# Copies of the running sum moved from the start of a down run into the duo ahead of it, and a sixth raw weight tile in a decoder trunk's feed-forward stage

## The chip, the core and the metric

The kernel runs on one core of a Trainium2 chip. Its engines are named as in the profile: PE (matrix products), PEld (PE's loading of the stationary operand), DVE (vector), ACT (scalar), POOL, and SP, whose queue issues the loads. The metric is the time of one execution of the whole program in microseconds (us): 2176.53 is the median of three runs of the kernel before (2175.78 to 2177.68).

## The reference, cut to what matters

A decoder trunk of two layers over 256 tokens of width 2048, in float32. Each layer has a mixer (gated linear attention in the first, differential attention over a shared K/V in the second) and a SwiGLU feed-forward stage, the FFN, with 5632 inner columns. The change touches the FFN, which runs twice:

```python
def swiglu(h, w_gate_up, w_down):
    gate, up = jnp.split(h @ w_gate_up, 2, axis=-1)
    return (jax.nn.silu(gate) * up) @ w_down
...
        f = swiglu(rmsnorm(x, pre_ffn_g[i]), ffn_w_gate_up[i], ffn_w_down[i])
        x = x + rmsnorm(f, post_ffn_g[i])
```

## The kernel before

**Numbers.** A float32 weight tile of 128x1024 is loaded by SP (`load`, L271) into one of NRAW = 5 buffers named `raw`. It is split into two parts: `hi`, a cast by ACT (L306), and `lo`, the rest, by DVE (L309). A product of a 128x128 piece of activations with a 128x512 piece of weights is three matmuls: hi by hi, hi by lo, lo by hi (L419 to L421 in `mm_act`, L559 to L561 in `triple`). Each `hi`/`lo` pair lies in a ring of NRING = 9, and `pump` keeps the splitting at most that far ahead of what PE has given free.

**Up steps.** The 5632 columns are 11 chunks of 512, numbered 0 to 10. Chunk 0 is done by `gated_first`. Each of the other ten is a *duo* (`gated_duo`, which calls `duo_seeded`): the gate chunk and the up chunk are worked together, in a scheme in which six of the eight slices of the depth (four in chunk 1) need seven products in place of eight. Such a fast slice is four weight parts, a to d, made by DVE additions (L341) of two raw tiles; part d is 128x512 and lies in narrower buffers, `hi5` and `lo5`, which take turns with two rooms in a spare tile (`self.narrow = (fp, 2, 2)`: four places in all). The sums of the duo stand in PSUM banks, which the code numbers 0 to 7. Behind the last fast slice, `early` takes the sums apart: ACT copies bank 0 into `sg` (L1270), and DVE does four additions (L1259), one of which writes into bank 7. The slices that are left (1 and 7) follow as plain products, and `late` finishes each bank as it is done.

**Down steps.** `ffn_steps` sets the order: up chunks in groups of two, with a down run of two output chunks behind most of them. A down run (`down_act`) multiplies the gated columns of one group with `w_down` and adds to what earlier groups gave. That running sum stands in SBUF, in `f`. So each output chunk begins with two copies by ACT, one for each half of the tokens, from `f` into two fresh PSUM buffers (L472), and the matmuls add onto these. At its end, ACT copies the sums back (L1335). The first group has no such copies. Of the down runs that have them, eight in each FFN stand behind a duo.

**What sets the order.** The code is recorded in the order in which it is written; then a scheduler sets the order on each engine, with priorities (`urgent`) and ties (`behind`: not ahead of a given instruction). On the chip each engine takes its own row in order: what stands behind a waiting instruction waits as well. SP's loads too are one row.

**Memory.** `fp` is a pool that is open during one FFN and lies where the mixer's pool lay before. PSUM has six buffers named `acc` and two named `tp`.

Of the kernel before, what the change touches and what calls it, by code (L numbers as in the profile page):

```python
# [11 lines left out]
F32 = mybir.dt.float32  # L12
# [6 lines left out]
P = 128  # L19
# [29 lines left out]
NRAW, NRING = 5, 9  # L49
# [147 lines left out]
class Trunk:  # L197
    def __init__(self, ctx, tc, t):
        self.ctx, self.tc, self.nc, self.t = ctx, tc, tc.nc, t

        def pool(name, **kw):
            return ctx.enter_context(tc.tile_pool(name=name, bufs=1, **kw))

        self.const = pool("const")
        self.big = pool("big")
        self.ring = pool("ring")
        self.hs = pool("hs")
        self.psum = pool("psum", space=bass.MemoryType.PSUM)
        self.dram = pool("dram", space=bass.MemoryType.DRAM)
        self.n = 0  # L210
        self.later = []
        self.stream = weight_stream()
        self.loads = load_list(self.stream)
        self.n_used = self.n_done = 0
        self.subs = {}
        self.split_off = None
        self.parts = {}
        self.raws = {}
        self.n_dma = self.n_conv = self.n_take = self.n_free = 0
        self.pool_lo = set()  # L220
        self.n_narrow = 0
        self.cap = 2
        self.ident = self.const.tile([P, P], F32, tag="ident", name="ident")
# [43 lines left out]

    def load(self):
        name, idx = self.loads[self.n_dma]
        raw = self.ring.tile([P, 1024], F32, tag="raw", name=self.uid("raw"), bufs=NRAW)  # L270
        self.nc.sync.dma_start(raw, self.t[name][idx])  # L271
        self.raws[self.n_dma] = raw
        self.n_dma += 1
# [28 lines left out]
    def split(self, src, gp=False):  # L302
        nc = self.nc
        w = src.shape[-1]
        hi, lo = self.places(w)
        cast = nc.scalar.copy(hi, src)  # L306
        eng = nc.gpsimd if gp else nc.vector
        with self.past(self.split_off):
            rest = eng.tensor_tensor(out=lo, in0=src, in1=hi.bitcast(F32), op=ALU.subtract)  # L309
        if not gp:  # L310
            self.parts[self.n_conv] = cast.ins, rest.ins
        return hi, lo
# [66 lines left out]

    def pump(self):  # L380
        n = len(self.stream)
        while self.n_conv < min(n, self.n_free + NRING, self.n_take + self.cap):
            self.convert()
            while self.n_dma < min(len(self.loads), self.n_done + NRAW):
                self.load()

    def take(self, name, idx, kind="plain"):
# [74 lines left out]
    def down_act(self, aT, w, s0, order, ns, evac, skew=0, base=None):  # L462

        ps, taken = {}, {}

        def run(u, b):
            c, s = order[u]
            if c not in ps:
                ps[c] = [self.acc(), self.acc()]
                if base:  # L470
                    for i in range(2):
                        self.nc.scalar.copy(ps[c][i], base(c, i))  # L472
            if not b:
                taken[u] = self.take(w, (c, s0 + s))
            self.mm_act(ps[c][b], aT, b, s, taken[u], ns, base is not None)
            if s == ns - 1:
                evac(c, b, ps[c][b])
            if b:
                self.free()
            self.tick()  # L480

        n = len(order) - skew
        for u in range(n):
            run(u, 0)
            run(u, 1)
        for b in range(2):
            for u in range(n, len(order)):
                run(u, b)

    def duo_seeded(self, aT, forms, fast, chunks, early, late):  # L490

        ps, held = {}, []
        (w1, n1), (w2, n2) = chunks

        def bank_of(bank):
            if bank not in ps:
                ps[bank] = self.tp().rearrange("p j t -> p (j t)") if bank in (2, 6) else self.acc()
                return True
            return False

        def add(bank, a, wp, j, last, onto=False):
            first = bank_of(bank)
            self.triple(ps[bank], a, wp, j, first and not onto, last, onto)

        def plain(bank, s, b, wp, last, onto=False):
            for j in range(2):
                add(bank, aT.tokens(2 * s + j, b), wp, j, last and j == 1, onto)
            if last:
                with self.behind(LATE_BEHIND):
                    late(bank, ps)  # L510
            self.tick()

        for s in range(7):
            k1, k2 = 2 * s, 2 * s + 1
            if s not in fast:
                wp = self.take(w1, (n1, s))
                for b, bank in enumerate((1, 3)):
                    plain(bank, s, b, wp, False)
                self.free()
                held.append(s)  # L520
                continue
            f, last = forms.pairs.index(s), s == fast[-1]
            plan = {
                "a": ((0, aT.tokens(k1, 0)), (1, aT.tokens(k2, 0))),
                "b": ((6, forms.fast(f, 2)), (2, forms.fast(f, 3))),
                "c": ((5, forms.fast(f, 1)), (3, aT.tokens(k2, 1))),
                "d": ((4, forms.fast(f, 0)),),
            }
            for kind, prods in plan.items():
                wp = self.take("duo", (*chunks, s), kind)  # L530
                for j, (bank, a) in enumerate(prods):
                    add(bank, a, wp, j, last and bank in (0, 4, 5, 6))
                self.free()
                if kind != "d":
                    self.tick()
            if last:
                bank_of(7)
                with self.behind(EARLY_BEHIND):
                    self.urgent(early)(ps)
        kept = [(s, self.take(w2, (n2, s))) for s in held]  # L540
        for s, wp in kept:
            plain(2, s, 0, wp, False)
        wp = self.take(w1, (n1, 7))
        for b, bank in enumerate((1, 3)):
            plain(bank, 7, b, wp, True)
        for s, wp2 in kept:
            plain(7, s, 1, wp2, False, True)
            self.free()
        self.free()
        wp = self.take(w2, (n2, 7))  # L550
        plain(2, 7, 0, wp, True)
        plain(7, 7, 1, wp, True, True)
        self.free()
# [696 lines left out]
        self.defer(5, lambda: next_gain(3))  # L1250
        self.chunk_act(aT, w, 3, 8, self.urgent(evac(3)), tail=SKEW)

    def gated_duo(self, hT, forms, w, c, rs, new_sg):

        nc = self.nc
        made = []
# [28 lines left out]
            else:  # L1285
                gated(1, ps[bank])

        self.duo_seeded(hT, forms, ffn_pairs(c), ((w, c), (w, 11 + c)), early, late)
        return made[0]

    def ffn(self, fp, hT, rs, gi, wgu, wd, post, after, name, reload, side=None):
        nc = self.nc
        self.narrow, self.n_narrow = (fp, 2, 2), 0
        forms = Forms(FAST_FFN, range(8), self.whole(4, [P, 4, 2, 4, P], f"{name}_fast", F32R))
        self.rest_of(forms, 2 * gi + 1, f"{name}_rest")
        temp = self.whole(5, [P, 4, C], f"{name}_temp")
# [45 lines left out]
        def part(c, b):  # L1342
            return f[0][:, b, c * C : (c + 1) * C]

        f = []
        plan = ffn_steps()
        for n, (kind, which, *chunks) in enumerate(plan):
            if kind == "up":
                sg = self.gated_duo(hT, forms, wgu, which, rs, new_sg) if which else gated_first()
                follow = plan[n + 1]  # L1350
                wait = 4 if which else 1
                if follow[0] == "down" and which not in follow[1]:
                    wait = 2 * len(down_order(*follow[1:])) + 1
                self.defer(wait, lambda sg=sg, c=which: gate_T(sg, c))
                continue
            chunks, skew = chunks[0], 0
            if not f:
                f.append(self.whole(5, [P, 2, D], name))
                if side:
                    self.defer(5, side)  # L1360
            if which == last:
                if chunks[0] == 0:
                    reload()
                else:
                    skew = LAST_SKEW
                for c in chunks:
                    gains[c] = self.gain(post, c)

            def done(c, b, ps, grp=which):
                if skew:  # L1370
                    self.urgent(evac)(grp, c, b, ps)
                else:
                    with self.behind(DOWN_BEHIND):
                        evac(grp, c, b, ps)

            base = None if which == first else part
            self.down_act(gTs[which], wd, 2 * which[0], down_order(which, chunks), 2 * len(which), done, skew, base)

    def values(self, vp, aT, rs, i, steps, every):

# [348 lines left out]
```

## Time and profile before

| | |
|---|---|
| runs of the kernel before, median (lowest to highest) | 2176.53 us (2175.78 to 2177.68) |
| the profiled execution | 2176.25 us |
| its span, first to last instruction | 2174.5 us |
| granted PE clock, mean | 0.999 |
| first FFN, second FFN, about | 385 to 1094 us, 1468 to 2174 us |
| raw loads of `w_gu`, of `w_d` | 352 and 176, 512 KB each, median 4.4 and 4.5 us to landing |
| ACT copies L472 | 80, 580 ns each (median) |

In rows of the timeline, the first two numbers are start and duration in us, then come engine, line, operation, output and inputs, and how many were merged; brackets hold the idle time of the engine ahead of it and what ended it. In rows of the waits stand the total, how often, and the longest. A matmul of 512 columns is drawn 0.39 us long, but the next one starts 0.23 us after it, so that rows of PE overlap.

### The profile page before, as it was taken

How to read it: one execution, taken by the hardware profiler on the slowest of the kernel's cores; microseconds unless marked ns; L12 is line 12 of the kernel's file. 1: busy time of each engine (PE TensorE's matmuls, PEld its weight loads, DVE VectorE, ACT ScalarE, POOL GpSimd, SP SyncE). 2: the span in 40 equal slices, each digit the busy share in tenths (PEclk: the TensorE clock that was granted, in tenths of full speed). 3: DMA queues.
4: the chain of work that ended last, by engine and by line, in shares of the span. 5: the costliest groups of instructions: out<-in, count | busy, mean ns of one | idle time of the engine just before them, and what ended most of it. 6: DMA issues, size and time to landing. Idle time of an engine off the chain costs nothing.

```text
span 2174.5 us, 28418 instructions
## 1 busy us (share of the span) xinstructions
PE 2153.9 (99%) x10044; PEld 1785.0 (82%) x10044; DVE 1942.6 (89%) x2666; ACT 1376.5 (63%) x1926; POOL 38.4 (2%) x66
## 2 busy tenths in 40 slices
PE   9999999999999999999999999999999999999998
PEld 7888788888888888888878888888888888888876
DVE  7989988999999999999798567889999999999996
ACT  8756655666666666666776455566656666666664
POOL 1000000000000000000000000000000000000000
PEclk9999999999999999999999999999999999999999
DMA  8545566566555666656767555465655556566664
GB/s 309 166 150 192 176 225 214 208 220 231 174 191 205 213 213 209 207 181 214 249 203 244 188 172 163 149 235 186 228 202 185 188 200 209 202 210 205 210 215 154
DMA packets 125043, 440.08 MB, mean 202 GB/s; under 512 B 14091, under 2 KB 16820, under 8 KB 123620
## 3 DMA queue, kind: packets, MB, share of 16 engines
q1 hardware_dynamic: 123724, 436.44, 59.3%
q10 hardware_dynamic: 1176, 1.84, 0.2%
q8 instruction: 78, 1.28, 0.2%
q14 instruction: 65, 0.53, 0.1%
HBM read 429.82 MB, written 9.97 MB: 202 GB/s over the span
## 4 chain that ended last, share of the span: by engine, by line
PE 88%; DVE 5%; DMA 3%; ACT 2%; issue 1%; SPq 0%; POOL 0%; ACTq 0%; DVEq 0%; POOLq 0%
PE acc L419 11%; PE acc L421 11%; PE acc L420 11%; PE acc L560 10%; PE acc L561 10%; PE acc L559 10%; PE acc L707 8%; PE acc L708 4%; PE tp L561 3%; PE tp L560 3%; PE tp L559 3%; DMA raw<-in_w_d_dram 2%; DVE lo L309 2%; ACT hi L306 2%; DVE raw L341 1%
## 5 line engine op out<-in xcount | busy, mean ns | idle before, releaser
L309 DVE TENSOR_TENSOR lo<-raw,hi 128x1024 fp32r<-128x1024 f32 x921 | 1098.4, 1218 | 131.3 <-ACT hi L306 125.8
L306 ACT CAST hi<-raw 128x1024 fp32r<-128x1024 f32 x923 | 946.9, 1051 | 376.5 <-PE acc L707 89.6
L419 PE MATMUL acc<-hi,f_ffn_gT 128*128 128x512 f32 x704 | 270.5, 392 | 6.1 <-ACT acc L472 6.0
L420 PE MATMUL acc<-lo,f_ffn_gT 128*128 128x512 f32 x704 | 272.6, 389 | 0.0
L421 PE MATMUL acc<-hi,f_ffn_gT 128*128 128x512 f32 x704 | 270.5, 389 | 0.0
L560 PE MATMUL acc<-lo,h_ffn 128*128 128x512 f32 x612 | 239.2, 391 | 0.1
L561 PE MATMUL acc<-hi,h_ffn 128*128 128x512 f32 x612 | 238.4, 390 | 0.0
L559 PE MATMUL acc<-hi,h_ffn 128*128 128x512 f32 x612 | 227.7, 389 | 0.0
L419 PEld LDWEIGHTS acc<-hi,f_ffn_gT 128*128 128x128 f32 x704 | 132.1, 188 | 38.6 <-ACT acc L472 11.1
L341 DVE TENSOR_TENSOR raw<-raw 128x512 f32<-128x512 f32 x232 | 159.2, 686 | 3.3
L421 PEld LDWEIGHTS acc<-hi,f_ffn_gT 128*128 128x128 f32 x704 | 132.2, 188 | 27.5
L420 PEld LDWEIGHTS acc<-lo,f_ffn_gT 128*128 128x128 f32 x704 | 132.2, 188 | 27.2
L560 PEld LDWEIGHTS acc<-lo,h_ffn 128*128 128x128 f32 x612 | 114.9, 188 | 26.2 <-DVE lo L309 1.0
L559 PEld LDWEIGHTS acc<-hi,h_ffn 128*128 128x128 f32 x612 | 114.9, 188 | 24.1
L561 PEld LDWEIGHTS acc<-hi,h_ffn 128*128 128x128 f32 x612 | 114.9, 188 | 23.1
L306 ACT CAST hi<-sum 128x512 fp32r<-128x512 f32 x72 | 44.8, 622 | 96.6 <-DVE sum L341 96.6
L306 ACT CAST f_ffn_rest<-sum 128x512 fp32r<-128x512 f32 x56 | 34.9, 623 | 95.6 <-DVE sum L341 95.6
L707 PE MATMUL acc<-h_q,hi 128*128 128x512 f32 x256 | 92.5, 401 | 0.0
L707 PE MATMUL acc<-h_kv,hi 128*128 128x512 f32 x256 | 90.7, 399 | 0.0
L707 PE MATMUL acc<-h_mix,hi 128*128 128x512 f32 x256 | 90.5, 398 | 0.0
L1335 ACT COPY f_ffn<-acc 128x512 f32<-128x512 f32 x80 | 46.7, 586 | 56.6 <-PE acc L421 56.1
L341 DVE TENSOR_TENSOR sum<-raw,raw 128x512 f32<-128x512 f32 x116 | 79.3, 683 | 0.1
(417 smaller groups left out, 4105.8 us busy)
## 6 DMA issues: line engine op xcount, KB each, us to landing
raw<-in_w_gu_dram SPq DMA_DIRECT2D x352, 512.0 KB, 4.4
raw<-in_w_d_dram SPq DMA_DIRECT2D x176, 512.0 KB, 4.5
raw<-in_gla_w_r_dram SPq DMA_DIRECT2D x32, 512.0 KB, 4.4
raw<-in_gla_w_v_dram SPq DMA_DIRECT2D x32, 512.0 KB, 4.0
raw<-in_gla_w_out_dram SPq DMA_DIRECT2D x32, 512.0 KB, 4.8
raw<-in_w_v_dram SPq DMA_DIRECT2D x32, 512.0 KB, 4.5
raw<-in_w_k_dram SPq DMA_DIRECT2D x32, 512.0 KB, 4.3
raw<-in_diff_w_q_dram SPq DMA_DIRECT2D x32, 512.0 KB, 3.5
```

The lines of the kernel that those rows point to most:

```text
L306: cast = nc.scalar.copy(hi, src)
L309: rest = eng.tensor_tensor(out=lo, in0=src, in1=hi.bitcast(F32), op=ALU.subtract)
L341: return self.nc.vector.tensor_tensor(out=out, in0=in0, in1=in1, op=ALU.add)
L419: nc.tensor.matmul(ps, ah, rh, start=(kt == 0 and not onto), stop=False, skip_group_check=onto)
L420: nc.tensor.matmul(ps, ah, rl, start=False, stop=False, skip_group_check=onto)
L421: nc.tensor.matmul(ps, al, rh, start=False, stop=(kt == 2 * ns - 1), skip_group_check=onto)
L559: nc.tensor.matmul(ps, ah, wh, start=first, stop=False, skip_group_check=onto)
L560: nc.tensor.matmul(ps, ah, wl, start=False, stop=False, skip_group_check=onto)
L561: nc.tensor.matmul(ps, al, wh, start=False, stop=last, skip_group_check=onto)
L707: nc.tensor.matmul(ps, lh, aT.both(kt), start=(kt == 0), stop=False)
L708: nc.tensor.matmul(ps[:, SEQ:], ll, aT.hi(kt), start=False, stop=(kt == KT - 1))
L1335: nc.scalar.copy(fc, ps)
```

## The change

The diff, without the lines that only pass an argument on:

```diff
     def load(self):
         name, idx = self.loads[self.n_dma]
-        raw = self.ring.tile([P, 1024], F32, tag="raw", name=self.uid("raw"), bufs=NRAW)
+        pool, bufs = self.ring, NRAW
+        if self.more_raw and name[:3] in ("w_g", "w_d"):
+            self.n_more += 1
+            if self.n_more % (NRAW + 1) == 0:
+                pool, bufs = self.more_raw, 1
+        raw = pool.tile([P, 1024], F32, tag="raw", name=self.uid("raw"), bufs=bufs)
...
-        cast = nc.scalar.copy(hi, src)
+        with self.past(self.led):
+            cast = nc.scalar.copy(hi, src)
...
     def pump(self):
         n = len(self.stream)
-        while self.n_conv < min(n, self.n_free + NRING, self.n_take + self.cap):
+        while self.n_conv < min(n, self.n_free + NRING, self.n_take + self.cap, self.open_to or n):
             self.convert()
-            while self.n_dma < min(len(self.loads), self.n_done + NRAW):
+            while self.n_dma < min(len(self.loads), self.n_done + NRAW + bool(self.more_raw)):
                 self.load()
...
             if c not in ps:
-                ps[c] = [self.acc(), self.acc()]
-                if base:
-                    for i in range(2):
-                        self.nc.scalar.copy(ps[c][i], base(c, i))
+                ps[c] = base(c) if base else [self.acc(), self.acc()]
+                self.led = None
...
-    def duo_seeded(self, aT, forms, fast, chunks, early, late):
+    def duo_seeded(self, aT, forms, fast, chunks, early, late, ahead):
...
+            if s == fast[-2]:
+                self.open_to = self.n_take + 8 + len(held) + 2
...
                 with self.behind(EARLY_BEHIND):
                     self.urgent(early)(ps)
+                self.open_to = None
+                ahead(0)
...
             plain(bank, 7, b, wp, True)
+        ahead(1)
...
     def ffn(self, fp, hT, rs, gi, wgu, wd, post, after, name, reload, side=None):
         nc = self.nc
-        self.narrow, self.n_narrow = (fp, 2, 2), 0
+        self.narrow, self.n_narrow = (fp, 1, 2), 0
+        self.more_raw, self.n_more = fp, 0
...
+        def seed(c, b):
+            ps = self.acc()
+            self.led = nc.scalar.copy(ps, part(c, b)).ins
+            return ps
...
+                def ahead(b, follow=follow):
+                    self.led = None
+                    if follow[0] == "down" and f and follow[1] != first:
+                        seeded.append(seed(down_order(*follow[1:])[0][0], b))
...
-            base = None if which == first else part
+            base = None if which == first else lambda c: [seeded.pop(0) if seeded else seed(c, b) for b in range(2)]
```

It has two parts. First, where a duo is followed by a down run with a running sum, the two copies for the run's first output chunk are recorded inside the duo: one behind `early`, one behind the last product of banks 1 and 3. Casts that are recorded after a copy are tied behind it (`led`), and no weight of the down run is split ahead of `early` (`open_to`). Second, in the FFN every sixth raw tile comes from the pool `fp`, so that six loads are open in place of five; the place for it is that of one narrow `hi5`/`lo5` pair, of which one is left beside the two rooms: three in turn in place of four. The later output chunks of a run get their copies where they had them.

The order is shown at the end of the duo of chunk 5 in the first FFN, which is followed by the down run of chunks 2 and 3; the fifteen other such places read alike around the first copy. On ACT, before, `sg` is the copy of bank 0, `hi_1006` to `hi_1012` are the last weight parts of the duo, `hi_1015` and those behind it parts of `w_down`, and `acc_1044` and `acc_1045` the two PSUM buffers of the first output chunk:

```order
L306 CAST hi_1006_5366<-raw_985_5263 128x1024
L1270 COPY sg_1034_5463<-acc_957_5152 128x512
L306 CAST hi_1009_5378<-raw_993_5297 128x1024
L306 CAST hi_1012_5390<-raw_996_5309 128x1024
L306 CAST hi_1015_5402<-raw_1002_5341 128x1024
L306 CAST hi_1018_5411<-raw_1005_5353 128x1024
L472 COPY acc_1044_5529<-f_ffn0_4436 128x512
L472 COPY acc_1045_5530<-f_ffn0_4436 128x512
L306 CAST hi_1021_5423<-raw_1008_5370 128x1024
```

On ACT, now, the last parts of the duo are `hi_1003` to `hi_1009`, those of `w_down` begin with `hi_1016`, and the two buffers are `acc_1015` and `acc_1034`:

```order
L314 CAST hi_1003_5364<-raw_979_5249 128x1024
L1281 COPY sg_1013_5425<-acc_954_5150 128x512
L314 CAST hi_1006_5376<-raw_982_5261 128x1024
L314 CAST hi_1009_5388<-raw_988_5293 128x1024
L1359 COPY acc_1015_5432<-f_ffn0_4438 128x512
L314 CAST hi_1016_5434<-raw_991_5305 128x1024
L314 CAST hi_1019_5440<-raw_997_5337 128x1024
L314 CAST hi_1022_5446<-raw_1000_5349 128x1024
L1359 COPY acc_1034_5492<-f_ffn0_4438 128x512
L314 CAST hi_1025_5452<-raw_1005_5368 128x1024
```

The first copy has moved ahead of two casts of `w_down` parts, and the second has moved behind one more of them.

On PE, before, at the same place: `acc_970` is a bank of the duo, `tp_964` its bank 2, and `acc_1044` and `acc_1045` the sums of the down run:

```order
L561 MATMUL acc_970_5202<-hi_1009_5378,h_ffn0_1_3491 128x512
L419 MATMUL acc_1044_5529<-hi_1015_5402,f_ffn0_gT2_5164 128x512
L560 MATMUL tp_964_5183<-lo_1013_5391,h_ffn0_1_3491 128x512
L561 MATMUL tp_964_5183<-hi_1012_5390,h_ffn0_1_3491 128x512
L559 MATMUL tp_964_5183<-hi_1012_5390,h_ffn0_1_3491 128x512
L560 MATMUL tp_964_5183<-lo_1013_5391,h_ffn0_1_3491 128x512
L561 MATMUL tp_964_5183<-hi_1012_5390,h_ffn0_1_3491 128x512
L419 MATMUL acc_1045_5530<-hi_1015_5402,f_ffn0_gT2_5164 128x512
L420 MATMUL acc_1044_5529<-lo_1016_5403,f_ffn0_gT2_5164 128x512
```

On PE, now, `acc_967` and `tp_961` are the same two banks of the duo, `acc_1012` is its bank 7, and `acc_1015` the first sum of the down run:

```order
L572 MATMUL acc_967_5200<-hi_1006_5376,h_ffn0_1_3491 128x512
L571 MATMUL tp_961_5181<-lo_1010_5389,h_ffn0_1_3491 128x512
L572 MATMUL tp_961_5181<-hi_1009_5388,h_ffn0_1_3491 128x512
L570 MATMUL tp_961_5181<-hi_1009_5388,h_ffn0_1_3491 128x512
L571 MATMUL tp_961_5181<-lo_1010_5389,h_ffn0_1_3491 128x512
L572 MATMUL tp_961_5181<-hi_1009_5388,h_ffn0_1_3491 128x512
L427 MATMUL acc_1015_5432<-hi_1016_5434,f_ffn0_gT2_5162 128x512
L570 MATMUL acc_1012_5424<-hi_1003_5364,h_ffn0_0_3490 128x512
L571 MATMUL acc_1012_5424<-lo_1004_5365,h_ffn0_0_3490 128x512
```

The first matmul of the down run has moved behind the five matmuls of bank 2, and behind it now stand the twelve of bank 7, which came later in the run before; the run's second matmul follows those twelve.

On SP, now, in the mixer ahead of the first FFN, `raw_702` is the first tile of the sixth buffer:

```order
L278 DMA raw_591_3219<-in_gla_w_out_dram 128x1024
L278 DMA raw_594_3231<-in_gla_w_out_dram 128x1024
L278 DMA raw_702_3833<-in_w_gu0_dram 128x1024
L278 DMA raw_597_3240<-in_gla_w_out_dram 128x1024
L278 DMA raw_600_3258<-in_gla_w_out_dram 128x1024
```

Before, `raw_597` followed `raw_594` directly; the load that now stands between them waits until PE has read the narrow buffers of the mixer's pool that lay in its place.

More of the change, by code (lines that the diff above doesn't have):

```diff
@@ L211, in __init__ @@
         self.later = []
+        self.more_raw, self.n_more = None, 0
+        self.open_to = self.led = None
         self.stream = weight_stream()
@@ L1251, in proj_out, with gated_duo @@
         self.chunk_act(aT, w, 3, 8, self.urgent(evac(3)), tail=SKEW)
-    def gated_duo(self, hT, forms, w, c, rs, new_sg):
+    def gated_duo(self, hT, forms, w, c, rs, new_sg, ahead):
         nc = self.nc
@@ L1286, in late @@
                 gated(1, ps[bank])
-        self.duo_seeded(hT, forms, ffn_pairs(c), ((w, c), (w, 11 + c)), early, late)
+        self.duo_seeded(hT, forms, ffn_pairs(c), ((w, c), (w, 11 + c)), early, late, ahead)
         return made[0]
@@ L1343, in part @@
             return f[0][:, b, c * C : (c + 1) * C]
+        def seed(c, b):
+            ps = self.acc()
+            self.led = nc.scalar.copy(ps, part(c, b)).ins
+            return ps
         f = []
+        seeded = []
         plan = ffn_steps()
@@ L1348, in ffn @@
             if kind == "up":
-                sg = self.gated_duo(hT, forms, wgu, which, rs, new_sg) if which else gated_first()
                 follow = plan[n + 1]
+                def ahead(b, follow=follow):
+                    self.led = None
+                    if follow[0] == "down" and f and follow[1] != first:
+                        seeded.append(seed(down_order(*follow[1:])[0][0], b))
+                sg = self.gated_duo(hT, forms, wgu, which, rs, new_sg, ahead) if which else gated_first()
+                self.led = None
                 wait = 4 if which else 1
@@ L1374, in done @@
                         evac(grp, c, b, ps)
-            base = None if which == first else part
+            base = None if which == first else lambda c: [seeded.pop(0) if seeded else seed(c, b) for b in range(2)]
             self.down_act(gTs[which], wd, 2 * which[0], down_order(which, chunks), 2 * len(which), done, skew, base)
+        self.more_raw = None
     def values(self, vp, aT, rs, i, steps, every):
```

## The prediction

> **What bounds the kernel now.** I read the page first, then the chain, then the waits of PE and of its weight loads, and then the timeline at the places that these name.
>
> ```profile
> span 2174.5 us, 28418 instructions
> PE 2153.9 (99%) x10044; PEld 1785.0 (82%) x10044; DVE 1942.6 (89%) x2666; ACT 1376.5 (63%) x1926; POOL 38.4 (2%) x66
> PE 88%; DVE 5%; DMA 3%; ACT 2%; issue 1%; SPq 0%; POOL 0%; ACTq 0%; DVEq 0%; POOLq 0%
> ```
>
> PE is busy in 99% of the span and carries 88% of the chain that ended last. Nothing can make this kernel faster by more than PE waits, unless it takes matmuls away, and the change takes none away. So the question is which of PE's waits go. Those that PE has on the copies are the largest that it has in the FFN:
>
> ```profile
> PE acc L419 <- ACT acc L472: 6.0, 9, 1.4
> PEld acc L419 <- ACT acc L472: 11.1, 13, 1.9
> PEld acc L560 <- DVE lo L309: 1.0, 2, 0.5
> ```
>
> PE waited nine times for a copy L472, 6.0 us in all. What one such wait costs is read from the starts of the matmuls, here at the end of chunk 5's duo, the place of the order rows above:
>
> ```profile
> 719.28 0.39 PE L561 MATMUL acc<-hi,h_ffn 128*128 128x512 f32 x1
> 719.99 0.50 PE L419 MATMUL acc<-hi,f_ffn_gT 128*128 128x512 f32 x1 [0.33 <-ACT acc L472]
> 720.33 0.40 PE L560 MATMUL tp<-lo,h_ffn 128*128 128x512 f32 x1
> 720.57 0.39 PE L561 MATMUL tp<-hi,h_ffn 128*128 128x512 f32 x1
> 720.79 0.40 PE L559 MATMUL tp<-hi,h_ffn 128*128 128x512 f32 x1
> 721.03 0.39 PE L560 MATMUL tp<-lo,h_ffn 128*128 128x512 f32 x1
> ```
>
> Undisturbed, a matmul starts 0.23 us after the one ahead of it (720.57 to 720.79). The L419 started 0.71 us after it, so the stop cost 0.48 us where the bracket says 0.33: the bracket counts from the drawn end, 0.39 us after the start, and so leaves out 0.16 us. The matmul behind the stop started 0.34 us later in place of 0.23, so that each stop costs another 0.11 us as PE takes up again. The reason stands on ACT:
>
> ```profile
> 713.42 0.58 ACT L1270 COPY sg<-acc 128x512 f32<-128x512 f32 x1
> 713.90 2.00 ACT L306 CAST hi<-raw 128x1024 fp32r<-128x1024 f32 x2
> 716.27 1.05 ACT L306 CAST hi<-raw 128x1024 fp32r<-128x1024 f32 x1 [0.37 <-DMA raw<-in_w_d_dram]
> 718.39 1.06 ACT L306 CAST hi<-raw 128x1024 fp32r<-128x1024 f32 x1 [1.07 <-DMA raw<-in_w_d_dram]
> 719.35 1.10 ACT L472 COPY acc<-f_ffn 128x512 f32<-128x512 f32 x2
> 720.39 2.04 ACT L306 CAST hi<-raw 128x1024 fp32r<-128x1024 f32 x2
> ```
>
> The PSUM buffer of the first copy was free at 714.0, when `sg` had been copied. But the copy stood behind two casts of `w_down` parts, and these waited for their loads. PE wanted the copy at 719.51.
>
> **The copies, a wait removed.** The nine listed stops cost 6.0 us plus nine times 0.16, 7.4 us. Two more are too short for the list:
>
> ```profile
> 970.76 0.39 PE L561 MATMUL acc<-hi,h_ffn 128*128 128x512 f32 x1
> 971.15 0.50 PE L419 MATMUL acc<-hi,f_ffn_gT 128*128 128x512 f32 x1
> 1865.07 0.39 PE L561 MATMUL acc<-hi,h_ffn 128*128 128x512 f32 x1
> 1865.56 0.50 PE L419 MATMUL acc<-hi,f_ffn_gT 128*128 128x512 f32 x1
> ```
>
> They are 0.39 and 0.49 us in place of 0.23, 0.4 us together. Eleven times 0.11 us for taking up again is 1.2 us. That makes 9.0 us at eleven of the sixteen places; at the other five PE did not stop. [...]
>
> Does the whole of it go? In the new order the first copy follows the two last casts of the duo, so that it runs at about 715.9 to 716.5, three us before PE wants it. What is late next, on that time scale? (1) The first down matmul stands five matmuls later, at 719.28 + 6 x 0.23 = 720.6, and its `hi`, cast by 717.3 before, comes 0.6 us later at most, behind the copy. (2) Behind it come the twelve matmuls of bank 7, from 720.9 on. Bank 7 is written by DVE, in this row:
>
> ```profile
> 719.82 0.69 DVE L1259 TENSOR_TENSOR acc<-acc,sg 128x512 f32<-128x512 f32 x1
> ```
>
> It ends at 720.5 even where it stands now, which leaves 0.4 us. (3) The second copy stands behind three casts, the third of which ended at 721.4 before; with 0.6 us for the copy it is ready at about 722.0, and PE wants it nineteen matmuls behind the first, at 724.9. The worst places for these are the two in which the loads of `w_d` are latest, ahead of the last group's runs, where SP also reloads `x`:
>
> ```profile
> 1033.20 0.39 PE L561 MATMUL acc<-hi,h_ffn 128*128 128x512 f32 x1
> 1035.03 0.50 PE L419 MATMUL acc<-hi,f_ffn_gT 128*128 128x512 f32 x1 [1.44 <-ACT acc L472]
> 1033.44 1.04 ACT L306 CAST hi<-raw 128x1024 fp32r<-128x1024 f32 x1 [2.98 <-DMA raw<-in_w_d_dram]
> 1034.39 1.10 ACT L472 COPY acc<-f_ffn 128x512 f32<-128x512 f32 x2
> 2117.68 0.50 PE L419 MATMUL acc<-hi,f_ffn_gT 128*128 128x512 f32 x1 [1.08 <-ACT acc L472]
> ```
>
> The first four rows are one of the two, the last is PE's row at the other. At the first the new order wants the first `hi` at 1033.20 + 6 x 0.23 = 1034.6, and the cast ended at 1034.5 with no help from a sixth tile. That is just enough, so I take the whole 9.0 us. That no `w_down` part is split ahead of `early` costs nothing: the first such cast ran at 716.27 before, behind the copy of `sg`. The copies are not more in number, and no weight part of the duo stands behind one. Each puts casts of the run 0.58 us later; the five matmuls and the twelve (3.9 us) give that time back.
>
> **The sixth raw tile.** It lets SP issue each load one tile earlier. ACT's waits for `w_d` come earlier by that, but PE does not stand behind them except through the copies. One other stop may go with it, in the last duo, where a load of `w_gu` came late:
>
> ```profile
> 2113.06 0.39 PE L561 MATMUL tp<-hi,h_ffn 128*128 128x512 f32 x1
> 2113.81 0.50 PE L559 MATMUL tp<-hi,h_ffn 128*128 128x512 f32 x1 [0.37 <-ACT hi L306]
> 2112.71 1.05 ACT L306 CAST hi<-raw 128x1024 fp32r<-128x1024 f32 x1 [1.51 <-DMA raw<-in_w_gu_dram]
> ```
>
> It is 0.75 - 0.23 + 0.11 = 0.6 us. No row shows whether one tile more suffices, so its worth lies between 0 and 0.6 us; I count 0.3. Its cost is on SP: the load that now stands among those of the mixer's last projection waits for PE's last read of a narrow pair, and loads queue behind it.
>
> ```profile
> 350.30 0.39 PE L561 MATMUL acc<-hi,f_mix_fast 128*128 128x512 f32 x1
> 348.37 4.60 SPq L271 DMA_DIRECT2D raw<-in_gla_w_out_dram  x3
> 354.79 1.05 ACT L306 CAST hi<-raw 128x1024 fp32r<-128x1024 f32 x1 [0.23 <-PE acc L561]
> 367.77 0.39 PE L419 MATMUL acc<-hi,gla_oT 128*128 128x512 f32 x1
> ```
>
> The first row is that last read, done at 350.7. The load behind, the second of the three, went out at about 349.5 (one of three in 4.6 us) and now goes at about 351, 1.5 us late. Its cast ran at 354.79, and PE first reads it at 367.77: 12 us hide it. Without that cover it would cost 1.5 us for each FFN, 3 in all.
>
> **The narrow pair less.** A pair is used anew after three fast slices in place of four.
>
> ```profile
> 695.55 0.62 ACT L306 CAST hi<-sum 128x512 fp32r<-128x512 f32 x1 [2.08 <-DVE sum L341]
> 703.15 0.39 PE L561 MATMUL acc<-hi,f_ffn_fast 128*128 128x512 f32 x1
> 702.24 0.62 ACT L306 CAST f_ffn_rest<-sum 128x512 fp32r<-128x512 f32 x1 [2.08 <-DVE sum L341]
> ```
>
> The pair that was cast at 695.55 is last read by the matmul at 703.15, 8 us later. Casts of part d follow each other in 6.7 us, so that the one that uses the pair again comes 20 us later. The 12 us between hide the loss: nothing.
>
> **The sum** for the profiled execution: 2176.25 - 9.0 - 0.3 = 2166.95. The runs' median lies 0.28 us above that execution, so I predict 2167.2 us.
>
> **The rivals.** A: the next operand is late at the two ends ahead of the last group, for the 0.1 us of margin there is thin and the reload of `x` may fall otherwise. Both stops then stay: 1.44 and 1.08 us with 0.16 + 0.11 each, 3.1 us; the time is 2170.3.
>
> B: DVE takes over as the bound.
>
> ```profile
> 720.00:782.00 62.00, 62.00 (x277) 51.37 (x278) 59.32 (x71) 40.61 (x49) 0.00 (x0) 1.00 0.59 201
> 782.00:845.00 63.00, 62.62 (x281) 51.41 (x279) 60.79 (x73) 40.97 (x51) 0.00 (x0) 1.00 0.60 204
> ```
>
> In these two stretches, a duo with its down run each, DVE (the fourth figure in us) is idle for 2.7 and 2.2 us, against 0.6 us that a stop costs on the mean. That speaks against it, but if this idle time lies where DVE cannot use it, the stops move to the ends of the duos and some 2 us are left of the gain: 2174.5.
>
> C: PE makes up for a stop behind it, and the kernel stays at 2176.5. The rows of 719.28 speak against it: once PE had its operands again the starts stayed 0.23 us apart. [...]
>
> D, slower: the cast of part d waits for PE at a narrow pair, and on ACT all casts behind it wait too. This decides from the point at which a pair is read later than 20 us after its cast, against the 8 us above. If each of the twenty duos lost 1 us by it, the time would be 2167.2 + 20 = 2187.
>
> **How the numbers follow.** Forecast 0.75, A 0.12, B 0.06, C 0.03, D 0.04. The range reaches from the forecast less 0.3 (the rest of the last duo's stop), less 0.75 (the runs' lowest against their median) and less 1.0 for the two waits of PEld on `lo` parts, 2165.1, to A plus 0.3 plus 1.15 (the runs' highest), 2171.8; that holds 0.87. Under 0.2% of the time, 4.4 us, a measurement of this kernel can hardly tell a difference from none. Forecast and A lie beyond it: faster 0.87. B and C lie within: 0.09. Slower: 0.04.
>
> **What would show it.** In the new profile PE's row of waits for the copies (their line is new) should be gone or under 1 us, the first down matmul of each run should start 0.23 us after the row ahead of it, and the two FFNs should be shorter by about 4.7 us each. A shows as a wait of PE on `hi` or on a copy in the last group; B as more waits of PE on `lo` at duo ends; D as ACT's casts of `sum` waiting for PE. The forecast is wrong if PE's stops in the FFN still add up to over 5 us, or if the waits go and the span does not follow.

## The result, and the profile after

The changed kernel takes 2166.35 us (median of 6 runs, 2165.60 to 2167.09), the kernel before 2177.11 us on the same chip (6 runs, 2175.78 to 2179.02). The ratio is 0.995, with a 95% interval of 0.9937 to 0.9963: faster by 10.8 us, or 0.5%. The forecast was 2167.2 us in a range of 2165.1 to 2171.8. The profiled execution took 2167.09 us.

The page of the changed kernel: the span, the busy times, and the chain that ended last.

```profile
span 2165.2 us, 28434 instructions
...
PE 2151.3 (99%) x10044; PEld 1786.8 (83%) x10044; DVE 1941.9 (90%) x2666; ACT 1373.2 (63%) x1926; POOL 37.1 (2%) x66
...
PE 96%; DVE 2%; ACT 1%; DMA 1%; issue 1%; SPq 0%; POOL 0%; DVEq 0%; POOLq 0%; ACTq 0%
```

The span is 9.3 us shorter with the same 10044 matmuls, and PE's share of the chain rises from 88% to 96%. What went is seen in PE's waits (total in us, times, longest); this is the whole list:

```profile
PE acc L429 <- DVE h_kv L789: 1.5, 2, 1.1
PE tp L783 <- DMA x_in<-in_x_dram: 1.2, 1, 1.2
PE acc L837 <- POOL ones L862: 1.1, 1, 1.1
PE acc L427 <- ACT diff_oT L1535: 0.7, 1, 0.7
PE acc L429 <- DVE h_ffn L789: 0.6, 2, 0.3
PE tp L570 <- ACT hi L314: 0.3, 1, 0.3
PE tp L783 <- ACT x_T L796: 0.3, 1, 0.3
```

The row for the copies, 6.0 us in nine waits, is gone, and no row of its size came in its place. At the end of chunk 5's duo ACT's and PE's rows now read:

```profile
713.71 0.58 ACT L1281 COPY sg<-acc 128x512 f32<-128x512 f32 x1
714.18 2.00 ACT L314 CAST hi<-raw 128x1024 fp32r<-128x1024 f32 x2
716.08 0.59 ACT L1359 COPY acc<-f_ffn 128x512 f32<-128x512 f32 x1
716.60 2.00 ACT L314 CAST hi<-raw 128x1024 fp32r<-128x1024 f32 x2
718.85 1.05 ACT L314 CAST hi<-raw 128x1024 fp32r<-128x1024 f32 x1 [0.25 <-DMA raw<-in_w_d_dram]
719.81 0.58 ACT L1359 COPY acc<-f_ffn 128x512 f32<-128x512 f32 x1
```

```profile
720.55 0.39 PE L571 MATMUL tp<-lo,h_ffn 128*128 128x512 f32 x1
720.77 0.39 PE L572 MATMUL tp<-hi,h_ffn 128*128 128x512 f32 x1
721.00 0.39 PE L427 MATMUL acc<-hi,f_ffn_gT 128*128 128x512 f32 x1
721.23 0.39 PE L570 MATMUL acc<-hi,h_ffn 128*128 128x512 f32 x1
```

The first copy ends at 716.7, and the down matmul (L427) that needs it starts at 721.00, 0.23 us after the row ahead of it: 4.3 us of spare, and no time lost behind it. At all sixteen places the first down matmul follows its predecessor by 0.23 us; at the two ends ahead of the last group the spare is 3.3 us. From its first matmul on `h_ffn` to its last on `f_ffn_gT`, the first FFN took 385.02 to 1084.14 before and takes 385.22 to 1079.48; the second took 1467.87 to 2165.88 and takes 1464.05 to 2156.52. That is 4.9 and 5.5 us shorter, 10.4 in all. Of these, 0.2 us are given back ahead of the first FFN and 0.8 between the two (383.73 us before, 384.57 now), which leaves the span's 9.3 to within 0.1. So the FFNs gained more than the span shows.

### The profile page after: what moved, and what is told of

It is laid out like the page before. It is cut to its first block, busy times and chain, and to the rows that moved or that the text cites. A ratio compares the mean times of both kernels' runs of the same rounds, so it can differ in the third digit from the quotient of the medians.

```text
span 2165.2 us, 28434 instructions
## 1 busy us (share of the span) xinstructions
PE 2151.3 (99%) x10044; PEld 1786.8 (83%) x10044; DVE 1941.9 (90%) x2666; ACT 1373.2 (63%) x1926; POOL 37.1 (2%) x66
## 4 chain that ended last, share of the span: by engine, by line
PE 96%; DVE 2%; ACT 1%; DMA 1%; issue 1%; SPq 0%; POOL 0%; DVEq 0%; POOLq 0%; ACTq 0%
PE acc L571 12%; PE acc L572 12%; PE acc L570 12%; PE acc L429 11%; PE acc L427 11%; PE acc L428 11%; PE acc L718 8%; PE acc L719 4%; PE tp L570 4%; PE tp L571 4%; PE tp L572 4%; PE tp L739 1%; DVE lo L317 1%; PE tp L783 1%; PE acc L1472 0%
## 5 line engine op out<-in xcount | busy, mean ns | idle before, releaser
L427 PE MATMUL acc<-hi,f_ffn_gT 128*128 128x512 f32 x704 | 267.5, 390 | 0.0
L427 PEld LDWEIGHTS acc<-hi,f_ffn_gT 128*128 128x128 f32 x704 | 132.0, 188 | 27.8 <-issue 0.6
L429 PEld LDWEIGHTS acc<-hi,f_ffn_gT 128*128 128x128 f32 x704 | 132.1, 188 | 27.4
L428 PEld LDWEIGHTS acc<-lo,f_ffn_gT 128*128 128x128 f32 x704 | 132.1, 188 | 27.4
L314 ACT CAST f_ffn_rest<-sum 128x512 fp32r<-128x512 f32 x76 | 47.3, 623 | 138.4 <-DVE sum L349 138.4
L570 PEld LDWEIGHTS acc<-hi,h_ffn 128*128 128x128 f32 x612 | 114.4, 188 | 23.6
L349 DVE TENSOR_TENSOR raw<-sum,raw 128x512 f32<-128x512 f32 x116 | 79.4, 684 | 0.0
```

Of the source, the lines that this page charges most:

```text
L349: return self.nc.vector.tensor_tensor(out=out, in0=in0, in1=in1, op=ALU.add)
L427: nc.tensor.matmul(ps, ah, rh, start=(kt == 0 and not onto), stop=False, skip_group_check=onto)
L428: nc.tensor.matmul(ps, ah, rl, start=False, stop=False, skip_group_check=onto)
L429: nc.tensor.matmul(ps, al, rh, start=False, stop=(kt == 2 * ns - 1), skip_group_check=onto)
L570: nc.tensor.matmul(ps, ah, wh, start=first, stop=False, skip_group_check=onto)
```

## The experiments

Two things change place in the rows: the copies on ACT, and on PE the first down matmul of a run, which now stands behind five matmuls of bank 2. Besides, loads come one tile earlier. The theory of the prediction (T) gave the gain to the copies' place on ACT. The rivals were that the loads give it (R), that PE makes up for stops anyway (C), that DVE is the next bound (B) and that the narrow pair costs (D). After the first runs another was added: it is PE's row that counts (P). The table holds what bears on T, R and P; "w_d casts ahead" says how many casts of `w_down` parts stand ahead of the first copy on ACT (at two of the sixteen places, the ends ahead of the last group, one fewer, where it isn't 0). Each ratio is to the kernel before on the same chip; its medians there lie between 2176.7 and 2177.9 us.

| kernel | first down matmul against bank 2's | w_d casts ahead | raw tiles | PE's waits at the first down matmul, us (times) | median us | ratio to before, 95% |
|---|---|---|---|---|---|---|
| before | ahead | 2 | 5 | 6.0 (9) | 2177.1 | 1 |
| changed | behind | 0 | 6 | none | 2166.4 | 0.9937 to 0.9963 |
| e1_ahead_only | behind | 0 | 5 | none | 2166.2 | 0.9935 to 0.9962 |
| e11_pe_order | behind | 2 | 5 | 0.4 (1) | 2169.5 | 0.9955 to 0.9979 |
| e2_sixth_only | behind at 14 of 16 | 3 | 6 | 1.8 (2) | 2170.2 | 0.9952 to 0.9977 |
| e5_copy_twice_before | behind | 2 | 5 | 1.5 (2) | 2170.8 | 0.9952 to 0.9977 |
| e12_act_order | held ahead | 0 | 5 | 2.6 (2) | 2171.4 | 0.9967 to 0.9986 |
| e14_sixth_hold | held ahead | 3 | 6 | 4.3 (5) | 2175.1 | 0.9982 to 1.0 |
| e13_hold | held ahead | 2 | 5 | 7.2 (10) | 2180.2 | 1.0007 to 1.0025 |

### The two parts of the change, each alone

**e1_ahead_only**, in the changed kernel:

```diff
-        self.narrow, self.n_narrow = (fp, 1, 2), 0
-        self.more_raw, self.n_more = fp, 0
+        self.narrow, self.n_narrow = (fp, 2, 2), 0
```

> The copies ahead, with five raw tiles and four narrow places as before. Theory T (the gain is the order of the copies on ACT): the eleven stops of PE go without the sixth tile too; 2177.1 less 9.0, about 2168 us, within 1 us, and PE waits for copies under 1 us in all. Theory R (the loads that come one tile earlier give the gain, whatever the order): half of the stops or more stay, 2172 us or more.

Measured: 2166.19 us (2165.99 to 2166.58), and no wait of PE for a copy. T holds: with the copies ahead, the sixth tile is worth nothing that can be measured.

**e2_sixth_only** is the kernel before with the diff's lines on `more_raw` and `(fp, 1, 2)`, and nothing else of it. The changed kernel without its tie `led`, or without `open_to`, has these same rows on ACT, PE and SP, so that both ties are needed for the copies to move.

> The sixth raw tile and the narrow pair less, with the copies recorded where they were. On ACT the two copies then stand behind three casts of w_down parts, one more than before, and the loads of these come one tile earlier. T: the one makes up for the other, and PE goes on waiting for the copies: 2177 us, give or take 3, with 4 us or more of such waits. R: the waits go, since the loads are earlier: 2170 us or less.

Measured: 2170.23 us (2167.96 to 2170.34), some 7 us less than T said. By its time R seemed to be right. But the copies came no earlier, for they stand behind one cast more. What had moved was PE's row: with later copies, the scheduler put the first down matmul behind bank 2's five, at fourteen places. PE's waits for copies in this kernel, in the profiled execution, which at 2167.96 us is the fastest of the five:

```profile
PE acc L425 <- ACT acc L478: 1.8, 2, 0.9
```

The two are the ends ahead of the last group, where the down matmul had stayed ahead. From this came theory P.

**e3_narrow_less** is the kernel before with `(fp, 1, 2)` in place of `(fp, 2, 2)`.

> One narrow pair less and nothing else. T: the 12 us of margin hide it, 2177.1 us within 0.5 us. Rival D (the cast of part d waits for PE at a narrow pair): slower by up to 1 us for each of the twenty duos, so 2179 to 2197 us.

Measured: 2176.98 us (11 runs, 2175.05 to 2178.74) against 2176.92, ratio 0.9991 to 1.0008. D falls: the pair less costs nothing.

### The copies left out, and made twice

**e4_copies_out** is the kernel before without the two copies for the first output chunk of every run that has them, eighteen runs in all. It leaves out the running sum of these chunks:

```diff
-                if base:
+                if base and ps.keys() - {c}:
...
-            self.mm_act(ps[c][b], aT, b, s, taken[u], ns, base is not None)
+            self.mm_act(ps[c][b], aT, b, s, taken[u], ns, base is not None and c != order[0][0])
```

> The kernel before without the copies of each down run's first output chunk: the running sum of that chunk is left out. T: PE's stops at these places go with the copies, 2177.1 less 9.0, about 2168 us, and no less by more than 1 us, since nothing else waits for them. Rival C (PE makes up for a stop behind it): no change, 2177 us. If the copies cost ACT time that PE feels where they now stand, this kernel is faster than the changed one by over 1 us.

Measured: 2166.19 us (2164.97 to 2166.70), 1.8 us less than T's 2168, where T allowed 1. Doing without these copies takes as long as moving them, but that equality is chance. In the profiled execution the two FFNs of e4 are only 6.4 us shorter than before, against 10.4 in the changed kernel, and another 3.2 us come from between the FFNs (380.47 us in place of 383.72), where the edit moves rows as well. So e4 can't say what the copies cost at their new place; what shows that nothing waits for them there is the list of PE's waits of the changed kernel. What e4 does show is that the waits for copies go with the copies, and what is late next while down matmuls still stand ahead of bank 2's on PE:

```profile
PE acc L419 <- ACT hi L306: 1.6, 2, 0.9
```

These are the first `w_down` casts at the two ends ahead of the last group.

**e5_copy_twice_before**: in the kernel before, the first copy of a run is made twice.

> The kernel before with the first copy of each down run behind a duo made twice, so that ACT is 0.58 us later there at sixteen places. T: at the eleven places where PE stops, each stop grows by 0.58 us, 6.4 us; at the five others the spare is used up first, so between 0 and 0.58 plus 0.11 us each, at most 3.5 us: 2183.5 to 2187 us. Rival C (PE makes up for a stop behind it): 2177 us, however long the waits are drawn.

Measured: 2170.75 us (2169.19 to 2172.29), 7 us faster than before, where T said 6 to 10 slower: a plain miss. As in e2, the scheduler had answered the longer copies by moving the first down matmul behind bank 2's five, here at all sixteen places. An edit on ACT was not an edit on ACT alone.

**e8_copy_twice_after**: in the changed kernel, the copy in `ahead(0)` is made twice.

> The changed kernel with the first copy made twice, the same work added at the same sixteen places; on ACT three copies then stand in a row, since the second copy comes between the two. T: they run while PE does the last matmuls of the duo, the first cast of the down run has 2 to 3 us of spare, and nothing is lost: 2166.4 us, at most 1 us more. Theory S (each microsecond of ACT at the end of a duo is paid by PE): 16 times 0.58, 9.3 us, so 2175.7 us.

Measured: 2169.32 us (2168.83 to 2170.18), ratio 0.9946 to 0.9971, which overlaps the changed kernel's. T said 1 us more at most, and the span grew by 1.9 us: a miss, if a small one. Two stops on late casts, one in the last duo of each FFN, make it up:

```profile
PE tp L570 <- ACT hi L314: 1.8, 2, 1.2
```

S, 9.3 us more, did not come. But this is no clean test of S, for here too the scheduler moved PE's row: at all sixteen places the first down matmul stands behind the twelve matmuls of bank 7 as well. At chunk 5's end it starts at 723.20; directly behind bank 2's five it would have started at 720.48. The first copy and its double end at about 716.9 there, so that they would have been in time for that as well; this is argued and was not run.

### PE's row and ACT's row, each alone

**e11_pe_order**, in the kernel before; ACT's, DVE's and SP's rows stay as they were, and PE's alone changes. `self.led` is the last matmul of bank 2, which `triple` notes in `self.two`:

```diff
+        self.two = []
         plain(2, 7, 0, wp, True)
+        self.led = self.two[-1]
+        self.two = None
...
-            self.mm_act(ps[c][b], aT, b, s, taken[u], ns, base is not None)
+            with self.past(self.led):
+                self.mm_act(ps[c][b], aT, b, s, taken[u], ns, base is not None)
+            self.led = None
```

> The kernel before with one tie: the first matmul of a down run stands behind the five matmuls of bank 2 on PE, as in the changed kernel. ACT's row is as before, word for word: the copies stand behind two casts of w_down parts. Theory T as predicted (the copies' place on ACT gives the gain): most of the stops stay, 2173 us or more. Theory P (found in the two runs in which PE's row moved by itself: it is PE's row that counts): five matmuls of 0.226 us are 1.13 us, more than eight of the eleven stops; of the other three (1.47, 1.60 and 1.25 us by the starts) 0.9 us stay, and 0.3 us of taking up again. 2177.1 less 7.8, about 2169.5 us.

Measured: 2169.52 us (2168.57 to 2171.45). Chunk 5's end on ACT and on PE, and PE's waits for copies:

```profile
718.08 1.06 ACT L307 CAST hi<-raw 128x1024 fp32r<-128x1024 f32 x1 [1.58 <-DMA raw<-in_w_d_dram]
719.04 1.11 ACT L473 COPY acc<-f_ffn 128x512 f32<-128x512 f32 x2
```

```profile
719.73 0.39 PE L567 MATMUL tp<-hi,h_ffn 128*128 128x512 f32 x1
719.96 0.74 PE L420 MATMUL acc<-hi,f_ffn_gT 128*128 128x512 f32 x2
```

```profile
PE acc L420 <- ACT acc L473: 0.4, 1, 0.4
```

The copies stand behind the two casts, and these wait for their loads, as before. The first copy ends at 719.6, and the matmul that needs it starts at 719.96, 0.23 us after the row ahead. P holds, and so does its number: five matmuls put ahead of the one that waits hide the wait without anything becoming faster. They don't hide all of it. At three of the eleven places PE still stops, among them for the second copy, whose matmul starts 0.52 us after its predecessor in place of 0.23. PE's row alone stays some 3 us behind the changed kernel.

**e12_act_order**: e1 with the first down matmul recorded ahead of bank 2's (in `ahead(2)`), which are tied behind it:

```diff
         wp = self.take(w2, (n2, 7))
-        plain(2, 7, 0, wp, True)
+        self.ahead_of = None
+        ahead(2)
+        with self.past(self.ahead_of):
+            plain(2, 7, 0, wp, True)
```

> The other half alone: the copies ahead on ACT as in the changed kernel, five raw tiles, and the first matmul of a down run held ahead of bank 2's matmuls on PE, as before (six of them stand behind it in place of five). T: the copies were ready 4.2 us before PE wanted them, and 2.9 us are left; the stops on copies go. The first w_down cast, ready 0.6 and 0.45 us ahead at the two ends before the last group, is then 0.75 to 0.9 us late: two stops on hi, 2 us in all; 2166.2 plus 2, about 2168 us. P: without the five matmuls the stops stay in the shape of waits on hi or on copies, 2173 us or more.

Measured: 2171.38 us (9 runs, 2169.76 to 2174.96). At chunk 5's end the down matmul started at 719.54 with no stop, 3.1 us after its copy. The copies are waited for nowhere. P said "without the five matmuls the stops stay in the shape of waits on hi or on copies, 2173 us or more"; nine of the eleven are gone, so it falls in this strict form. The two stops on `hi` that T named are there, the second much longer than the 0.9 us that T gave it, and T's 2168 us is missed by 3.4 (the hold itself costs as much, as the next runs show):

```profile
PE acc L1381 <- ACT hi L315: 2.6, 2, 1.9
```

**e13_hold** and **e14_sixth_hold** hold the matmul in the same way, with the copies recorded behind the duo; e14 has the sixth tile besides.

> A control: the first matmul of each down run is held ahead of bank 2's matmuls on PE by a tie, and the copies stand on ACT behind two casts of w_down parts, both as before; five raw tiles. It should be the kernel before: 2177 us within 1.5, with some 6 us of waits of PE for copies. If it is faster, the tie itself gives something, and what was read from the run that held the same order with the copies ahead falls.

> The control with the sixth raw tile and the narrow pair less; on ACT the copies stand behind three casts of w_down parts. P and T (the row on PE and the row on ACT decide, each for itself; earlier loads alone don't): PE wants the copies as early as before, and they come no earlier, since one cast more stands ahead of them; 2177 us, give or take 3. R (what the sixth tile gave alone came from the loads): 2171 us or less, the waits for copies mostly gone.

Measured: 2180.24 us (11 runs, 2178.63 to 2183.56) and 2175.08 us (11 runs, 2173.50 to 2177.07). PE's waits for copies, e13 and then e14:

```profile
PE acc L1384 <- ACT acc L1365: 7.2, 10, 1.7
```

```profile
PE acc L1385 <- ACT acc L1366: 4.3, 5, 1.4
```

The control was to take 2177 us within 1.5; it is 3.5 us slower than before, so the hold is not free. Its trace shows what it costs, here at chunk 5's end, with the row of PEld's waits on `lo`:

```profile
716.98 0.39 PE L579 MATMUL tp<-hi,h_ffn 128*128 128x512 f32 x1
717.32 0.50 PE L578 MATMUL acc<-lo,h_ffn 128*128 128x512 f32 x1
717.65 0.39 PE L579 MATMUL acc<-hi,h_ffn 128*128 128x512 f32 x1
```

```profile
PEld acc L578 <- DVE lo L318: 5.9, 16, 0.4
```

The hold leaves one more matmul of bank 2 behind the down matmul. So PE comes to a `lo` part one matmul earlier, and DVE has not finished it: the next two starts are 0.34 and 0.33 us apart in place of 0.23. That is 0.22 us at each of the sixteen places, 3.5 us in all, too short at each for PE's own list. The kernel before has such a wait at two of them, 0.7 us together, so the hold adds 2.8 us. The rows of e12 and e14 have the same sixteen waits, so the control takes them out of the comparison.

Against the control, the copies' place on ACT alone is worth 8.9 us by the medians (e12) and 6.0 between the two profiled executions. The sixth tile alone is worth 5.2 and 3.0 us (e14). By its time e14 lies where P and T put it, and R's 2171 us is missed; but R is partly right, for five of the ten waits go though one cast more stands ahead of the copies.

### DVE and the size of a stop

**e9_dve_2** and **e10_dve_6** are the changed kernel with two and six additions more behind the last result of each duo, written to a buffer that nobody reads:

```diff
                 gated(1, ps[bank])
+                for _ in range(2):
+                    op(v, sg[:, 0, :], sg[:, 0, :], ALU.subtract)
```

> The changed kernel with two idle DVE additions of 128x512 (0.67 us each) behind the last result of each duo, 1.3 us of DVE a duo. DVE was idle for 2.15 us in each stretch of 62 us. T: they go into that idle time: 2166.4 us, at most 2 us more. Rival B (DVE is the bound now, its idle time lies where it can't use it): 20 times 1.3, 27 us, so 2193 us.

> The same with six such additions, 4.0 us a duo, 1.9 us more than DVE's idle time. T: 1.9 us for each of the twenty duos, 37 us slower, 2203 us within 8. Rival B: 20 times 4.0, 2247 us. If DVE has other room, 2166 to 2180 us.

Measured: 2181.20 us and 2204.09 us (ratios 1.0007 to 1.0025 and 1.0105 to 1.0132). Groups of DVE and waits of PE, e9 and then e10:

```profile
L1270 DVE TENSOR_TENSOR hs<-sg 128x512 f32<-128x512 f32 x40 | 27.4, 685 | 0.0
```

```profile
PE acc L570 <- ACT hi L314: 7.3, 17, 0.9
PE tp L570 <- ACT hi L314: 2.8, 2, 1.7
```

```profile
L1270 DVE TENSOR_TENSOR hs<-sg 128x512 f32<-128x512 f32 x120 | 82.1, 684 | 0.1
```

```profile
PE tp L570 <- ACT hi L314: 12.2, 18, 0.7
PE acc L570 <- ACT hi L314: 11.4, 24, 0.6
```

e9 lies between the theories: 27.4 us of DVE work lengthen the span by 14.5 us, 0.7 us for each duo, though each stretch of 62 us had 2.15 us idle. So some 0.6 of the 1.4 us a duo were taken in, and the rest of the idle time lies where work at a duo's end can't use it: DVE still shows 1.8 us of it in 62 (mean of three stretches). With six (37.3 us, 1.9 for each duo) the forecast from the idle time came out, but in part by luck, since it took the idle time to be used up first, and 1.0 us in 62 is left even here. e10 also answers C. Its waits are 23.6 us in 42 stops; with 0.16 and 0.11 us for each stop, as the prediction counts them, that is 34.9 us, and the span grew by 37.3. PE makes up for nothing that can be seen, and the idle times alone would be 14 us short.

## Why the prediction was right, and where its reasons were not

**The size of the stops: right, and its last tenth luck.** The sum of 9.3 us (9.0 for eleven stops, 0.3 for the sixth tile) against the profiled execution met the span's 9.3. But the FFNs gave 10.4 and the rest of the program took 1.0 back. Beside the 9.0 of the copies, the last duo's stop went (0.6 us) and one like it came (0.6 us, below). The two waits of PEld on `lo`, which the prediction put only into its range, went too, 0.7 us by the starts. The other 0.7 us lies in no single stop that was found. The two corrections, 0.16 us that the bracket leaves out and 0.11 us of taking up again, carry 2.6 of the sum; without them it would have been 6.7. e10 bears the two corrections out with other stops.

**Whether all of it goes: right, with the place well read.** The first copy was put at 715.9 to 716.5 and ran at 716.08 to 716.67. At the ends ahead of the last group the margin was given as 0.1 us. With five raw tiles (e1) the first `hi` was ready 0.6 and 0.45 us ahead; with six, 2.35 us. So rival A was near in kind: in e12, where PE wants these casts 1.4 us earlier (six matmuls of 0.23 us), the stops are there, 2.6 us in two.

**The cause: only one of two.** The prediction explained the gain by the copies' place on ACT, and used the five matmuls on PE only as cover for the first `hi`. The step that fails is "The reason stands on ACT". PE's row alone is worth 7.2 us (e11: 2169.5 against 2176.7 on the same chip), and ACT's row alone 8.9 against its control, by the medians. Each takes away most of the waits for copies without the other, and neither reaches the whole gain. They don't add up, because they remove the same waits: the change has both, and gains 10.8.

**The sixth tile: near in its size, with a cost left out.** It was counted at 0.3 us and gives nothing that can be measured beside the copies (e1). The stop that it was to shorten, at 2113.81, did go. But one of the same kind came in the other FFN's last duo:

```profile
1027.77 0.39 PE L572 MATMUL tp<-hi,h_ffn 128*128 128x512 f32 x1
1028.46 0.50 PE L570 MATMUL tp<-hi,h_ffn 128*128 128x512 f32 x1 [0.30 <-ACT hi L314]
```

That is 0.69 - 0.23 + 0.11 = 0.6 us. The words "PE does not stand behind them except through the copies" were right, and for that very reason the tile is worth 5.2 us while the copies wait (e14). The prediction didn't price that case, since the change doesn't leave the copies there. Nor did it price what the tile costs between the two FFNs. All six kernels here that have it take 384.3 to 384.6 us there, and all that have five tiles take 383.7, except e4 (380.5): 0.8 us, with a second wait of PE on `h_kv`. Which row of the tail makes that wait is open.

**What was costed at nothing** was nothing that can be measured: the narrow pair (e3), and the copies at their new place, for which no row of PE's waits is left. SP's load ahead of the first FFN can't be told from nothing either: that FFN starts 0.2 us later, and over all the kernels here its start scatters by 0.9 us, with six tiles and with five.

**The rivals.** B did not come, but it is nearer than 2.15 us of idle time sound: 1.4 us more at a duo's end already stop PE (e9). C falls with e10, D with e3. No kernel here beats the changed one by more than can be measured; e1 equals it with less code.

## What to carry to other kernels

The wait between ACT's row and PE's was taken away on either row: by letting the awaited copies start earlier (e12, 8.9 us against its control), or by putting other ready matmuls ahead of the one that waits (e11, 7.2 us). Look on both sides before giving the gain to one, for the two remove the same wait and did not add up: together they gave 10.8 us. Where a scheduler orders the rows, an edit on one engine can move another (in e5 and e8 a copy more on ACT moved PE's first down matmul at all sixteen places), so compare the rows of every experiment before reading its time.

## What the runs showed of the hardware

In the profiled execution of e12 PE's granted clock was 0.50 from 2113 to 2116 us, behind a stop of 1.86 us. The rows, and the stretches around them (PEclk is the third figure from the end of a row):

```profile
2110.44 0.39 PE L579 MATMUL acc<-hi,h_ffn 128*128 128x512 f32 x1
2112.69 0.66 PE L1381 MATMUL acc<-hi,f_ffn_gT 128*128 128x512 f32 x1 [1.86 <-ACT hi L315]
2113.15 0.63 PE L577 MATMUL tp<-hi,h_ffn 128*128 128x512 f32 x1
2113.57 0.63 PE L578 MATMUL tp<-lo,h_ffn 128*128 128x512 f32 x1
...
2116.13 0.47 PE L578 MATMUL acc<-lo,h_ffn 128*128 128x512 f32 x1
2116.44 0.40 PE L579 MATMUL acc<-hi,h_ffn 128*128 128x512 f32 x1
```

```profile
2109.00:2112.00 3.00, 1.83 (x9) 1.16 (x7) 2.16 (x3) 0.60 (x2) 0.00 (x0) 1.00 1.02 412
...
2113.00:2116.00 3.00, 3.00 (x8) 2.33 (x8) 2.76 (x4) 3.00 (x5) 0.00 (x0) 0.50 0.76 258
```

After 1.86 us of waiting the starts were 0.43 us apart for 3.4 us, at a granted clock of 0.50. By an estimate from these starts (eight, 0.2 us each) that cost some 1.6 us beyond the stop, and in the profiled execution it is part of what e12 took beyond T's 2168. In e9 a stop of 1.67 us was nearly as long. Behind it the first start came 0.34 us later and the next 0.23, at a granted clock of 1.00:

```profile
2118.35 0.39 PE L572 MATMUL tp<-hi,h_ffn 128*128 128x512 f32 x1
2120.41 0.50 PE L570 MATMUL tp<-hi,h_ffn 128*128 128x512 f32 x1 [1.67 <-ACT hi L314]
2120.75 0.39 PE L571 MATMUL acc<-lo,h_ffn 128*128 128x512 f32 x1
2120.98 0.40 PE L572 MATMUL acc<-hi,h_ffn 128*128 128x512 f32 x1
```

```profile
2120.00:2121.00 1.00, 0.59 (x3) 0.51 (x4) 0.61 (x1) 1.00 (x3) 0.00 (x0) 1.00 1.01 401
2121.00:2124.00 3.00, 3.00 (x15) 2.47 (x14) 3.00 (x5) 3.00 (x4) 0.00 (x0) 1.00 0.90 336
```

So the two stops, 1.86 us and 1.67 us long, were followed by granted clocks of 0.50 and 1.00. No run here shows what lowered the clock in e12.
